# One core, two decoder blocks: the pooling mixer's padded chunks move to the convolution's tiles, and its modulation columns to its second half

## The chip, the cores and the metric

The kernel runs on one core of a Trainium2 chip. The metric is device time in microseconds (us) for one execution. A core has TensorE (matrix products, PE in the profile), VectorE (DVE), ScalarE (ACT), GpSimd (POOL) and SyncE (SP, which here only issues transfers). The engines run side by side, each works through its own instructions in the order in which the program holds them, and they wait for each other through semaphores.

## The reference

The input is one sequence of 512 tokens with 1024 channels. A first block applies two mixers to it, each behind a modulated norm; a second block applies attention, retention and a feed-forward part. Only the borders of the pooling mixer matter here. Cut to that:

```
sh, sc, gt = split(silu(c) @ w_mod[i] + b_mod[i])        # "modulation": one vector per block
h = rms(x, norm_g[i]) * (1 + sc) + sh

# mixer 0, convolution
a, b, g = split(h @ w_in);  y = depthwise_conv31(a * sigmoid(b)) + db
x += gt * ((silu(layernorm(y)) * silu(g)) @ w_out)

# mixer 1, pooling
v, g = split(h @ w_in)                                   # 1024 channels each
pooled = stack(window_mean(v_k, w) for w in (2, 4, 8, 16)) - v
y = (pooled @ w_grp per group) * scale
x += gt * ((y * silu(g)) @ w_out)
```

The second block's modulation is a product of the same kind, of its own vector silu(c_2) with 48 x 128 columns.

## The kernel before

Channels lie on the 128 partitions and the 512 tokens along them, so an activation of 1024 channels is eight tiles, called chunks here. Every matrix product is made of three TensorE passes, high half by high half, high by low and low by high: `mm3`, lines 307 to 309. Weights arrive in groups of eight 128 x 128 blocks (`w`, 512 KB); ScalarE makes the high half of a group (`whi`, line 291) and VectorE the low half (`wlo`, line 296). Three groups are held. `group_steps` writes these two instructions for the group that is two ahead of the one that TensorE reaches, so they stand in ScalarE's and VectorE's order at the start of each chunk.

**Pooling mixer.** Its input product has 16 output chunks of 24 matmuls each; chunks 0 to 7 are `v` and 8 to 15 are the gate. Chunks 0 to 2 are finished by the function `crossing`, and a loop makes 3 to 15, chunk by chunk, in four PSUM tiles in turn (two named `m`, two `z`). Weight group and chunk have the same number here. `ev_pl` takes a chunk out of PSUM: for chunks 0 to 7 ScalarE copies it (line 903) into a tile with eight zero columns at either end, which VectorE writes (lines 901 and 902), and `pool_chunk` makes running sums on GpSimd (line 888: one for window 2, two for 4, three for 8, four for 16), multiplies by the reciprocal count (GpSimd, line 891), subtracts the chunk (VectorE, line 892) and splits the result (VectorE, lines 379 and 380). For chunks 8 to 15 ScalarE applies the sigmoid-weighted gate (line 908). After chunk 15 come four groups of two outputs, 48 matmuls over two weight groups; `ev_g` takes each output out of PSUM on VectorE (line 920), and the output product follows (line 352 and on).

**Modulation columns.** `gemv` makes 128 of them: a transfer of 512 KB into one of two tiles `gw` (line 254) and a product with reduction on VectorE (line 255). 96 are needed in all, some called up at each step by `need`; the pooling mixer's loop calls for numbers 40 to 55, which are sixteen. Number 48 is the first that belongs to the second block: before its product the tile `cb` is loaded anew by a transfer that may start only when number 47's product is done (line 210), and ScalarE applies silu to it (line 211).

**Tiles.** The first two mixers share the pools of `Phase("A", ...)`. Pool `y` has four tiles: the convolution's padded inputs for VectorE and GpSimd, then the pooling mixer's padded chunks and its running sums. Pool `e` has 14 tiles of 272 numbers: for each of the five chunks that TensorE convolves two raw halves (line 649 on), two high and two low halves.

The engines' order in the convolution and the crossings is written by hand; in the pooling mixer's loop a scheduler sets it from the order of the code, the waits and its own estimates.

Of the kernel before, what the change touches and what calls it, by code (L numbers as in the profile page):

```python
# [9 lines left out]
F32 = mybir.dt.float32  # L10
F32R = mybir.dt.float32r
# [4 lines left out]
T = 512  # L16
# [115 lines left out]
def body(ctx: ExitStack, tc, ap, out):  # L132
# [12 lines left out]
    def nm(p):  # L145
        uid[0] += 1
        return f"{p}{uid[0]}"
# [11 lines left out]
        def close(self):  # L159
            self.stack.close()  # L160

    phase = [Phase("A", {"y": 4, "e": 14, "p": 2, "dg": 6, "v": 2, "c": 10, "a": 20, "z": 2, "d": 2})]

    def at(tag="a", dt=F32, n=T):
        return phase[0].pool[tag].tile([P, n], dt, tag=tag, name=nm(tag))
# [16 lines left out]
    def f(x):  # L182
        return x.bitcast(F32)

    mm = nc.tensor.matmul
    V, A, G = nc.vector, nc.scalar, nc.gpsimd
# [55 lines left out]
    done, pace = [0], [0]  # L242

    def gemv():
        i = done[0]
        if i >= 96:
            return
        done[0] += 1
        if i == 48:
            cb.append(silu_c("c_2"))  # L250
        j = MOD_ORDER[i]
        with tc.high_priority(offset=3000):
            t = gst.tile([P, D], F32, tag="g", name=nm("gw"))
            nc.sync.dma_start(out=t, in_=ap["wmod"][j])
        product = V.tensor_tensor_reduce(  # L255
            out=t, in0=t, in1=cb[-1], scale=1.0, scalar=bias_of(j),
            op0=ALU.mult, op1=ALU.add, accum_out=mod[:, j:j + 1])
        tc.keep_in_program_order(product)

    def need(n):  # L260
        while done[0] < n:
            gemv()
# [57 lines left out]
    def lin(src, ms, kn, evac, halves=False, acc=acc):  # L320

        if not halves:
            for m in ms:
                o = acc()
                for k in range(kn):
                    mm3(o, block(0), src[k], k == 0, k == kn - 1)
                    at_block[0] += 1
                evac(m, o, 0, T)
            return
        for a in (0, T // 2):  # L330
            b = a + T // 2
            for i, m in enumerate(ms):
                o = acc()
                for k in range(kn):
                    mm3(o[:, a:b], block(i * kn + k), cols(src[k], a, b), k == 0, k == kn - 1)
                evac(m, o, a, b)
        at_block[0] += len(ms) * kn
# [38 lines left out]
    def split_in(t, a=0, b=T, into=None, eng=None, n=T, tag="a"):  # L376

        hi, lo = into or (at(tag, F32R, n), at(tag, F32R, n))
        V.tensor_copy(out=hi[:, a:b], in_=t[:, a:b])
        (eng or V).tensor_tensor(out=lo[:, a:b], in0=t[:, a:b], in1=f(hi[:, a:b]), op=ALU.subtract)  # L380
        return hi, lo
# [171 lines left out]
    WE = H2 + 16  # L553
    ytile, yc, cv = {}, {}, {}
# [82 lines left out]
    def ev_in(m, o, a, b):  # L637
        if m < 8:
            pending[m] = o
            return  # L640
        if m < 16:
            i = m - 8
            s = at()
            A.activation(out=s, in_=o, func=AF.Sigmoid)  # L644
            v = pending.pop(i)
            if i in ON_PE:
                ytile[i] = []
                for g in range(2):
                    y = at("e", F32, WE)
                    V.memset(y[:, 0:8], 0.0)  # L650
                    V.memset(y[:, 7 + H2:WE], 0.0)
                    for p in range(2):
                        V.tensor_tensor(out=y[HALF[p], 7 + p:7 + p + H2], in0=v[HALF[g], p:T:2], in1=s[HALF[g], p:T:2], op=ALU.mult)
                    ytile[i].append(split_in(y, 0, WE, n=WE, tag="e"))
                return
            y = at("y", F32, WY)
            V.memset(y[:, 0:HALO], 0.0)
            V.memset(y[:, HALO + T:WY], 0.0)
            V.tensor_tensor(out=y[:, HALO:HALO + T], in0=v, in1=s, op=ALU.mult)
            ytile[i] = y  # L660
            return
        t = at()
        A.activation(out=t, in_=o, func=AF.Silu)
        pending[m] = t
# [134 lines left out]
    with tc.manual_schedule(engines=HAND):  # L799
# [29 lines left out]
        for _ in rsqrt_steps(pr(), [sq.acc], D, 0, T, n0.rb):  # L829
            next(work)  # L830
        lead[0] = 1
        lin_k(h0, CV_FIRST, KC, ev_in)
        lead[0], ahead[0] = LEAD, 1
        engine = {"V": V, "A": A, "G": G}
# [4 lines left out]
        for act in PLAN:  # L839
            kind, n, on = re.fullmatch(r"([a-z])(\d*)([A-Z]*)", act).groups()  # L840
            n = int(n or 1)
            if kind == "l":
                lin(n0.h, (n,), KC, lambda m, o, a, b: raw.update({m: o}), acc=pm)
            if kind == "x" or kind == "l" and n < 8:
                ev_in(n, raw.pop(n), 0, T)
            elif kind in running:
                for _ in range(n):
                    next(running[kind], 0)
            elif kind == "b":
                for _ in range(n):  # L850
                    early.append(diagonals(*later.pop(0), [engine[e] for e in on]))
            elif kind == "g":
                need(done[0] + n)
            elif kind == "c":
                conv_end(n, engine[on])
            elif kind == "s":
                next(stats)
            elif kind == "z":
                z_norm(n, engine[on])
            elif kind == "y":  # L860
                z_gate(n, *[engine[e] for e in on])
            elif kind == "m":
                next(products)
# [17 lines left out]
    def pool_chunk(m, v):  # L881
        w = WINDOWS[m // 2]

        W = T + 16
        cur, n = v, 1
        while n < w:
            s = at("y", F32, W)
            G.tensor_tensor(out=s[:, 0:W - 2 * n + 1], in0=cur[:, 0:W - 2 * n + 1], in1=cur[:, n:W - n + 1], op=ALU.add)
            cur, n = s, 2 * n
        t = at("c")  # L890
        G.tensor_tensor(out=t, in0=cur[:, 8 - w // 2:8 - w // 2 + T], in1=cnt[m // 2], op=ALU.mult)
        V.tensor_sub(out=t, in0=t, in1=v[:, 8:8 + T])
        pooled[m] = split_in(t)

    vt = {}

    def ev_pl(m, o, a, b):
        if m < 8:
            if m not in vt:
                vt[m] = at("y", F32, T + 16)  # L900
                V.memset(vt[m][:, 0:8], 0.0)
                V.memset(vt[m][:, 8 + T:16 + T], 0.0)  # L902
            A.copy(out=vt[m][:, 8 + a:8 + b], in_=o[:, a:b])
            if b == T:
                pool_chunk(m, vt.pop(m))
        else:
            t = at("dg" if m < 12 else "a")
            A.activation(out=t, in_=o, func=AF.Silu)
            sg[m - 8] = t

    for m, o in enumerate(first):
        ev_pl(m, o, 0, T)
    for m in range(len(first), 16):
        lin(n1.h, (m,), KC, ev_pl)
        need(done[0] + (2 if m < 6 else 1))
    z1 = [None] * KC

    def ev_g(m, o, a, b):
# [298 lines left out]
    def lin_tok():  # L1217

        os = [pz() if j < 2 else pm() for j in range(4)]
        for k in range(KC):  # L1220
            wh, wl = block(0, 4)
            at_block[0] += 4
            for j, o in enumerate(os):
                hh, hl = cols(h[k], j * P, j * P + P)
                mm(o, hh, wh, start=k == 0, stop=False)  # L1225
                mm(o, hh, wl, start=False, stop=False)  # L1226
                mm(o, hl, wh, start=False, stop=k == KC - 1)  # L1227
        return [split(o) for o in os]
# [99 lines left out]
    for hd in range(RET_HEADS):  # L1328
# [3 lines left out]
        v = lin_tok()  # L1332
# [168 lines left out]
```

## Time and profile before

| | us |
|---|---|
| median of 3 runs (lowest to highest) | 1681.62 (1677.55 to 1683.55) |
| the profiled execution's own time | 1682.93 |
| its span, first to last instruction | 1681.2 |
| TensorE busy in the span | 1601.3 (95%) |
| VectorE busy | 1036.3 (62%) |
| GpSimd busy | 500.6 (30%) |
| pooling mixer, chunk 3 to the first matmul of line 352 | 329.77 to 425.39 |

The span lacks the 1.7 us in which nothing of the core is recorded, before and after. Shares are means over stages with very different limits, so the stage's own rows count. In a timeline, a row is: start, duration, engine, line, operation, output from input, number merged, and in brackets the idle time ahead of it and what ended it.

### The profile page before, as it was taken

Reading aid. Unit: us, or ns where it says so; the run is one execution under the profiler, and the core shown is the slowest. Engines: PE = TensorE matmul, PEld = TensorE weight load, DVE = VectorE, ACT = ScalarE, POOL = GpSimd, SP = SyncE. Lnnn points to the kernel's source line nnn. Section 1 sums busy time; section 2 is a strip of 40 time slices with the busy share of each in tenths; the row PEclk is TensorE's granted clock in tenths of the full one; section 3 lists DMA queues with packets and bytes.
Section 4 is the critical chain, followed back from the end, with each engine's and each line's share of the span. In section 5 each row is a group of like instructions: output and inputs, shape, how many; then the busy total and the mean of one; then the engine's idle time right before and its main releaser. Section 6 shows DMA issues by size and latency. Waiting matters only on the chain.

```text
span 1681.2 us, 20261 instructions
## 1 busy us (share of the span) xinstructions
PE 1601.3 (95%) x7904; PEld 1351.6 (80%) x7904; DVE 1036.3 (62%) x1449; ACT 596.2 (35%) x920; POOL 500.6 (30%) x370
## 2 busy tenths in 40 slices
PE   6888898979999999999999999999999999999997
PEld 4677787968888878878888888888888888888887
DVE  6899988796678887886567554633254533333222
ACT  4422443523356566542332212223333422222221
POOL 2758635571124544550030201204441100000001
PEclk9999999989999999999999999999999999999999
DMA  8542334247521111225546332322322332332321
GB/s 273 163 151 68 109 126 144 76 150 248 191 76 51 52 62 51 72 67 165 167 153 203 95 118 71 96 89 74 99 91 85 101 92 96 100 100 90 99 89 62
DMA packets 54578, 187.64 MB, mean 112 GB/s; under 512 B 6097, under 2 KB 8273, under 8 KB 54482
## 3 DMA queue, kind: packets, MB, share of 16 engines
q1 hardware_dynamic: 52498, 183.20, 34.0%
q10 hardware_dynamic: 1984, 3.15, 0.6%
q8 instruction: 62, 1.02, 0.3%
q14 instruction: 34, 0.28, 0.1%
HBM read 184.22 MB, written 2.10 MB: 111 GB/s over the span
## 4 chain that ended last, share of the span: by engine, by line
PE 68%; DVE 18%; ACT 6%; issue 4%; POOL 3%; DMA 1%; SPq 0%; POOLq 0%; DVEq 0%; ACTq 0%
PE m L307 9%; PE m L308 9%; PE m L309 9%; PE z L307 7%; PE z L309 7%; PE z L308 7%; DVE wlo L296 4%; DVE gw L255 2%; DVE d L573 2%; ACT whi L291 1%; DVE dg L527 1%; PE m L1227 1%; PE z L1227 1%; PE z L1226 1%; PE m L1225 1%
## 5 line engine op out<-in xcount | busy, mean ns | idle before, releaser
L296 DVE TENSOR_TENSOR wlo<-w,whi 128x1024 fp32r<-128x1024 f32 (+1 forms) x243 | 329.8, 1360 | 341.4 <-ACT whi L291 340.5
L291 ACT CAST whi<-w 128x1024 fp32r<-128x1024 f32 x244 | 255.2, 1049 | 633.6 <-PE m L308 269.1
L307 PE MATMUL m<-h,whi 128*128 128x512 f32 x730 | 288.5, 395 | 4.6 <-ACT a L644 2.0
L309 PE MATMUL m<-h,wlo 128*128 128x512 f32 x730 | 286.5, 392 | 1.7 <-DVE y L902 1.4
L308 PE MATMUL m<-h,whi 128*128 128x512 f32 x730 | 286.1, 392 | 1.9 <-POOL h L480 1.9
L307 PEld LDWEIGHTS m<-h,whi 128*128 128x128 f32 x730 | 138.1, 189 | 36.0 <-ACT a L644 2.2
L309 PEld LDWEIGHTS m<-h,wlo 128*128 128x128 f32 x730 | 138.1, 189 | 32.3 <-DVE y L902 1.9
L308 PEld LDWEIGHTS m<-h,whi 128*128 128x128 f32 x730 | 137.8, 189 | 29.6 <-POOL h L480 2.2
L309 PE MATMUL z<-h,wlo 128*128 128x512 f32 x338 | 133.9, 396 | 7.1 <-DVE y L902 7.0
L307 PE MATMUL z<-h,whi 128*128 128x512 f32 x338 | 133.7, 395 | 0.0
L308 PE MATMUL z<-h,whi 128*128 128x512 f32 x338 | 133.2, 394 | 0.0
L397 POOL TENSOR_TENSOR c<-c,c 128x512 f32<-128x512 f32 x10 | 13.4, 1336 | 370.2 <-ACT c L435 370.0
L397 POOL TENSOR_TENSOR s<-s,s 128x512 f32<-128x512 f32 x14 | 18.7, 1333 | 321.0 <-ACT s L1265 292.2
L255 DVE CUSTOM_DVE_ANT_0 gw<-gw,cb,vec 128x1024 f32<-128x1024 f32 x64 | 92.2, 1448 | 20.3 <-DMA gw<-in_wmod 13.4
L1041 POOL TENSOR_TENSOR s<-s,s 128x512 fp32r<-128x512 f32 x64 | 92.7, 1458 | 30.7 <-DVE s L1040 30.7
L309 PE MATMUL z<-a,wlo 128*128 128x512 f32 (+1 forms) x222 | 81.7, 368 | 1.5 <-DVE wlo L296 1.5
L309 PEld LDWEIGHTS z<-h,wlo 128*128 128x128 f32 x338 | 64.7, 191 | 22.0 <-DVE y L902 7.8
L307 PE MATMUL z<-a,whi 128*128 128x512 f32 (+1 forms) x222 | 82.1, 370 | 0.0
L308 PE MATMUL z<-a,whi 128*128 128x512 f32 (+1 forms) x222 | 81.5, 367 | 0.0
L307 PEld LDWEIGHTS z<-h,whi 128*128 128x128 f32 x338 | 64.8, 192 | 13.3
L308 PEld LDWEIGHTS z<-h,whi 128*128 128x128 f32 x338 | 64.7, 191 | 13.4
L307 PE MATMUL m<-a,whi 128*128 128x512 f32 (+1 forms) x196 | 71.5, 365 | 0.0
(415 smaller groups left out, 3539.8 us busy)
## 6 DMA issues: line engine op xcount, KB each, us to landing
w<-in_weights SPq DMA_DIRECT2D x244, 512.0 KB, 3.7
gw<-in_wmod SPq DMA_DIRECT2D x96, 512.0 KB, 4.2
x<-in_xt SPq DMA_DIRECT2D x8, 256.0 KB, 4.5
s<-in_dec ACTq DMA_DIRECT2D x4, 256.0 KB, 3.6
out_x<-h SPq DMA_DIRECT2D x4, 256.0 KB, 2.5
p<-in_cnt ACTq DMA_DIRECT2D x2, 256.0 KB, 2.6
v<-in_cnt ACTq DMA_DIRECT2D x2, 256.0 KB, 3.2
cb<-in_c SPq DMA_DIRECT2D x1, 512.0 KB, 6.5
```

What stands on the lines that cost most here:

```text
L255: product = V.tensor_tensor_reduce(out=t, in0=t, in1=cb[-1], scale=1.0, scalar=bias_of(j), op0=ALU.mult, op1=ALU.add, accum_out=mod[:, j:j ...
L291: A.copy(out=hi, in_=w)
L296: e.tensor_tensor(out=lo[:, part], in0=w[:, part], in1=f(hi[:, part]), op=ALU.subtract)
L307: mm(o, l[0], r[0], start=first, stop=False)
L308: mm(o, l[0], r[1], start=False, stop=False)
L309: mm(o, l[1], r[0], start=False, stop=last)
L397: self.eng.tensor_tensor(out=n, in0=self.acc, in1=t, op=ALU.add)
L527: engs[s].tensor_tensor(out=t.rearrange("p (a b) -> p a b", a=8), in0=diag.unsqueeze(1).to_broadcast([P, 8, P // 2]), in1=dws[s][:, c:c + ...
L573: V.scalar_tensor_tensor(out=cv[i], in0=y[:, j:j + T], scalar=tap(i, j), in1=cv[i], op0=ALU.mult, op1=ALU.add)
L1041: G.tensor_tensor(out=lo[:, 0:w], in0=t[:, 0:w], in1=f(hi[:, 0:w]), op=ALU.subtract)
L1225: mm(o, hh, wh, start=k == 0, stop=False)
L1227: mm(o, hl, wh, start=False, stop=k == KC - 1)
```

## The change

The raw halves of the TensorE convolution go to pool `c` (ten tiles, shared with norms and the convolution's results), and a high and a low half share one tile of pool `e`, which now has seven tiles of 544 numbers. The pooling mixer's padded chunks go to `e`, and `y` keeps the running sums alone. The loop over chunks 3 to 15 calls for no modulation column up to chunk 7 and for two after each of chunks 8 to 15 (before: two after chunks 3 to 5, one after each later one); there are sixteen either way. From line 650 on, lines of the changed kernel stand one higher.

```
-    phase = [Phase("A", {"y": 4, "e": 14, "p": 2, "dg": 6, "v": 2, "c": 10, "a": 20, "z": 2, "d": 2})]
+    phase = [Phase("A", {"y": 4, "e": (7, 2 * 272), "p": 2, "dg": 6, "v": 2, "c": 10, "a": 20, "z": 2, "d": 2})]
...
-                    y = at("e", F32, WE)
+
+                    y, e = at("c"), at("e", F32R, 2 * WE)
...
-                    ytile[i].append(split_in(y, 0, WE, n=WE, tag="e"))
+                    ytile[i].append(split_in(y, 0, WE, into=(e[:, 0:WE], e[:, WE:2 * WE])))
...
-                vt[m] = at("y", F32, T + 16)
+                vt[m] = at("e", F32, T + 16)
...
-        need(done[0] + (2 if m < 6 else 1))
+        need(done[0] + (2 if m >= 8 else 0))
```

VectorE's order in the first half, before, from the low half of weight group 6 to that of group 7. The L892 row subtracts chunk 3, and the two L379 and L380 rows split it; each `gw` row is a modulation column.

```order
L296 TENSOR_TENSOR wlo_3014<-w_2959,whi_3013 128x1024
L901 MEMSET y_3041 128x8
L902 MEMSET y_3041 128x8
L892 TENSOR_TENSOR c_2997<-c_2997,y_2989 128x512
L379 CAST a_3000<-c_2997 128x512
L380 TENSOR_TENSOR a_3001<-c_2997,a_3000 128x512
L255 ISA gw_3004,mod<-gw_3004,cb_144,vec 128x1024
L255 ISA mod 128x1
L255 ISA gw_3007,mod<-gw_3007,cb_144,vec 128x1024
L255 ISA mod 128x1
L296 TENSOR_TENSOR wlo_3068<-w_3011,whi_3067 128x1024
```

The same place in the changed kernel:

```order
L296 TENSOR_TENSOR wlo_2998<-w_2949,whi_2997 128x1024
L893 TENSOR_TENSOR c_2987<-c_2987,e_2979 128x512
L379 CAST a_2990<-c_2987 128x512
L380 TENSOR_TENSOR a_2991<-c_2987,a_2990 128x512
L296 TENSOR_TENSOR wlo_3046<-w_2995,whi_3045 128x1024
```

The two columns are gone from between the two weight groups, and so are the memsets, which now stand in the convolution. The same five rows follow for chunks 4, 5 and 6; the first two columns come behind the low half of group 10.

VectorE's order at the end of the loop, before, from the low half of the first `w_grp` group (`wlo_3447`) to the first output of `ev_g` (L920):

```order
L296 TENSOR_TENSOR wlo_3447<-w_3408,whi_3446 128x1024
L255 ISA gw_3476,mod<-gw_3476,cb_3257,vec 128x1024
L255 ISA mod 128x1
L296 TENSOR_TENSOR wlo_3483<-w_3444,whi_3482 128x1024
L255 ISA gw_3512,mod<-gw_3512,cb_3257,vec 128x1024
L255 ISA mod 128x1
L296 TENSOR_TENSOR wlo_3519<-w_3480,whi_3518 128x1024
L920 SCALAR_TENSOR_TENSOR c_3528<-m_3515,vec,dg_3255 128x512
```

The same stretch in the changed kernel, where `wlo_3431` belongs to the first `w_grp` group:

```order
L296 TENSOR_TENSOR wlo_3431<-w_3389,whi_3430 128x1024
L255 ISA gw_3424,mod<-gw_3424,cb_3379,vec 128x1024
L255 ISA mod 128x1
L255 ISA gw_3460,mod<-gw_3460,cb_3379,vec 128x1024
L255 ISA mod 128x1
L296 TENSOR_TENSOR wlo_3470<-w_3428,whi_3469 128x1024
L255 ISA gw_3463,mod<-gw_3463,cb_3379,vec 128x1024
L255 ISA mod 128x1
L255 ISA gw_3499,mod<-gw_3499,cb_3379,vec 128x1024
L255 ISA mod 128x1
L296 TENSOR_TENSOR wlo_3509<-w_3467,whi_3508 128x1024
L255 ISA gw_3502,mod<-gw_3502,cb_3379,vec 128x1024
L255 ISA mod 128x1
L921 SCALAR_TENSOR_TENSOR c_3518<-m_3505,vec,dg_3221 128x512
```

Five columns stand there where two stood, and the last of the sixteen is the row just ahead of the first output of `ev_g`.

ScalarE's order around the new `cb`, in the changed kernel (`whi_3391` is the high half of weight group 15, `m_3346` is chunk 12):

```order
L909 ACTIVATE dg_3338<-z_3307 128x512
L211 ACTIVATE cb_3379<-cb_3379 128x1024
L909 ACTIVATE a_3377<-m_3346 128x512
L291 CAST whi_3391<-w_3347 128x1024
```

Before, `cb` stood behind the gate of chunk 9 and ahead of the high half of weight group 13; now it stands behind that of chunk 11 and ahead of the high half of group 15.

## Rows read from the trace of the kernel before

**Rows 1.** The page's first part: TensorE's busy time, share and instructions.
```profile
PE 1601.3 (95%) x7904; PEld 1351.6 (80%) x7904; DVE 1036.3 (62%) x1449; ACT 596.2 (35%) x920; POOL 500.6 (30%) x370
```

**Rows 2.** Windows: length, busy time by engine, TensorE's granted clock, DMA share.
```profile
351.61:381.21 29.60, 21.16 (x74) 16.14 (x72) 29.29 (x33) 4.81 (x7) 21.46 (x15) 0.83 0.56 173
...
414.51:425.39 10.88, 10.88 (x50) 9.01 (x48) 10.03 (x14) 6.08 (x9) 3.99 (x3) 1.00 0.65 226
```

**Rows 3.** TensorE's timeline, chunks 7 to 10 and the output product's first matmul.
```profile
355.24 0.80 PE L309 MATMUL z<-h,wlo 128*128 128x512 f32 x1 [3.02 <-DVE y L902]
355.83 0.63 PE L307 MATMUL z<-h,whi 128*128 128x512 f32 x1
...
363.91 0.50 PE L309 MATMUL m<-h,wlo 128*128 128x512 f32 x1 [1.45 <-DVE y L902]
...
373.63 0.80 PE L309 MATMUL z<-h,wlo 128*128 128x512 f32 x1 [3.98 <-DVE y L902]
...
381.21 0.39 PE L307 MATMUL m<-h,whi 128*128 128x512 f32 x1
...
425.39 0.39 PE L352 MATMUL m<-a,whi 128*128 128x512 f32 x1
```

**Rows 4.** VectorE's timeline, low halves of groups 6 and 7 and between them.
```profile
342.18 2.09 DVE L296 TENSOR_TENSOR wlo<-w,whi 128x1024 fp32r<-128x1024 f32 x1
...
346.40 1.54 DVE L892 TENSOR_TENSOR c<-c,y 128x512 f32<-128x512 f32 x1 [2.09 <-POOL c L891]
347.97 1.17 DVE L379 CAST a<-c 128x512 fp32r<-128x512 f32 x1
349.18 1.42 DVE L380 TENSOR_TENSOR a<-c,a 128x512 fp32r<-128x512 f32 x1
350.52 2.31 DVE L255 CUSTOM_DVE_ANT_0 gw<-gw,cb,vec 128x1024 f32<-128x1024 f32 x1
...
353.97 1.22 DVE L296 TENSOR_TENSOR wlo<-w,whi 128x1024 fp32r<-128x1024 f32 x1
```

**Rows 5.** GpSimd: its wait for padded chunks (300 to 400 us), and its timeline.
```profile
POOL y L888 <- DVE y L902: 11.0, 4, 3.8
...
355.36 4.04 POOL L888 TENSOR_TENSOR y<-y 128x527 f32<-128x527 f32 x3 [3.61 <-DVE y L902]
...
373.75 6.27 POOL L888 TENSOR_TENSOR y<-y 128x527 f32<-128x527 f32 x4 [1.26 <-DVE y L902]
380.10 2.16 POOL L891 TENSOR_TENSOR c<-y,p 128x512 f32<-128x512 f32 x1
```

**Rows 6.** VectorE's timeline, second half of the loop and the first output of `ev_g`.
```profile
394.58 1.29 DVE L255 CUSTOM_DVE_ANT_0 gw<-gw,cb,vec 128x1024 f32<-128x1024 f32 x1 [6.93 <-ACT cb L211]
...
399.64 1.29 DVE L255 CUSTOM_DVE_ANT_0 gw<-gw,cb,vec 128x1024 f32<-128x1024 f32 x1 [1.42 <-DMA gw<-in_wmod]
...
416.71 0.75 DVE L920 SCALAR_TENSOR_TENSOR c<-m,vec,dg 128x512 f32<-128x512 f32 x1
```

**Rows 7.** Timelines of SP's queue and of ScalarE: the new `cb`.
```profile
386.92 0.43 SPq L210 DMA_DIRECT2D cb<-in_c  x1
...
393.49 1.06 ACT L211 ACTIVATE cb<-cb 128x1024 f32<-128x1024 f32 x1 [10.77 <-DMA cb<-in_c]
```

**Rows 8.** Transfers issued at 395.9, 397.1, 408.5 and 386.9: size, issue to landing.
```profile
gw<-in_wmod SPq DMA_DIRECT2D x1, 512.0 KB, 3.6
...
gw<-in_wmod SPq DMA_DIRECT2D x1, 512.0 KB, 4.2
...
gw<-in_wmod SPq DMA_DIRECT2D x1, 512.0 KB, 5.5
...
cb<-in_c SPq DMA_DIRECT2D x1, 512.0 KB, 6.5
```

**Rows 9.** TensorE in the convolution: a wait, and the window behind it.
```profile
123.72 0.58 PE L307 MATMUL z<-e,dg 128*128 128x256 f32 x1 [5.64 <-DVE dg L527]
...
123.70:129.70 6.00, 5.98 (x27) 5.83 (x28) 5.97 (x4) 2.87 (x4) 5.92 (x4) 0.50 0.39 131
```

## The prediction

> **What bounds the kernel now.** The page's first part comes first: TensorE is busy for 95% of the span [rows 1], so the most that any edit can win lies in the few places where it stands still or runs below its full clock. The second look is the granted clock by windows [rows 2]: from 351.61 to 381.21 it is 0.83 and TensorE is busy for 21.16 of 29.60 us, while VectorE is busy for 29.29; from 414.51 to 425.39 TensorE is busy throughout at 1.00. Third, TensorE's timeline [rows 3] says where the loss sits: waits of 3.02, 1.45 and 3.98 us ahead of the low half of a weight group, for chunks 7, 8 and 9. The first is put down to a memset (line 902) that had long been done; the low half `wlo` on VectorE starts at 353.97 and takes 1.22 [rows 4], so it ends at 355.19, and TensorE goes on at 355.24.
>
> What is lost can be counted. Chunk 10 starts at 381.21 and line 352 at 425.39 [rows 3]. The last stretch holds 48 matmuls in 10.88 us [rows 2], 0.2267 each, so a chunk of 24 takes 5.44. From 381.21, six chunks and that stretch should take 43.52, and took 44.18: only 0.66 is lost late. Chunks 7 to 9 should take 16.32 and took the 29.60 of the first window: 13.28 lost, 8.45 in the three waits and 4.83 in a clock below full behind the two longer ones (0.83 over the window).
>
> VectorE is late because its work for a chunk, beside GpSimd, is `wlo` 2.09, L892 1.54, the cast 1.17, line 380 1.42, and two columns of up to 2.31 [rows 4]: 8 to 9 us against 5.44. And it also waits 2.09 for GpSimd there, which for its part waits 11.0 in all for padded chunks [rows 5], since in the old order the memsets into a `y` tile stand behind VectorE's other work.
>
> **The change, early part: tiles and columns.** The convolution keeps its instructions; its raw halves lie in another pool, and eight pairs of memsets join it on VectorE, where they wait until TensorE has read an `e` tile. A pass over 512 columns costs 1.17 [rows 4] and eight columns are a 64th of it, so the work is near 0, under a TensorE that is busy 95% of the span [rows 1]. Of the waits I know the bounds alone: nothing where VectorE comes later than TensorE, and the 5.64 of a wait in the convolution [rows 9] where it comes first, with the rest of VectorE's evictions queued behind. I take 0, because TensorE's convolution of a chunk is over before VectorE splits the next in the order of the code, and leave the other end to the slower rival below. The four-fold wait of GpSimd (11.0 us, [rows 5]) goes. Its last instruction ended at 382.26 (380.10 plus 2.16); without waits that is 371.3. Chunk 7's own sums and product are 6.27 plus 2.16, so chunk 6 is done there at 362.8.
>
> VectorE then never waits for GpSimd long, and runs beside it nearly always. One period is 1.54 + 1.17 + 1.42 + 2.09 = 6.22 us [rows 4], against TensorE's 5.44. The low half of group 6, at 342.18, comes later: some six instructions ahead of it, which ran beside an idle GpSimd, now run beside a busy one, and each loses about what `wlo` does (2.09 less 1.22, 0.87), some 4.7 us in all, less than 6 x 0.87 because the shorter ones lose less. That ends it near 349.0, and four more periods of 6.15 to 6.22 bring the first column to 373.6 at the latest; bounded from below it is chunk 6's end plus a period, 369.0. I take C = 372.5, nearer the upper end because the rows show contention in each instruction. TensorE reads a low half some 0.6 us into a chunk (355.24 less 3.02 is 352.22, chunk 7 began at 351.61), so it starts chunk 10 at about 371.6, **9.6 us earlier** than 381.21. Its 3.7 us above seven bare chunks from 329.77 come in waits of 0.6 to 2 us, and the 1.45 of chunk 8 left the clock at full.
>
> **The late part: sixteen columns behind one another.** All have to be done between C and the first L920, which in the new order stands right behind the last. A product takes 1.2 to 1.29 [rows 6]. A tile freed at 395.87 was read again at 399.64, and loads took 3.6 and 4.2, once 5.5 [rows 8]; so I count 4.1 us from a product's end to the next product on that tile (3.6 and 4.2, each with the 0.15 us between landing and reading). The products from C on, each with its end:
>
> - 1 and 2 (loaded ahead): C+2.4; chunk 7's finish 1.8 (L892 and the split, without GpSimd), a `wlo` of 1.2: C+5.4. Numbers 3 and 4 end at C+6.6 and +7.8, `wlo` +9.0.
> - 5 and 6: read at +10.7 (6.6 + 4.1) and +11.9, ending at +13.1; `wlo` +14.3. 7 and 8: +17.2 and +18.4.
> - Then `cb`. Its transfer may start only now: 0.5 for the issue (row 0.43), 6.57 from issue at 386.92 to silu at 393.49, silu 1.06 [rows 7]. S = C+26.5, that is 399.0. Both engines get past it: ScalarE has the high half of group 15 behind it.
> - 9 and 10: S+2.4; `wlo` of group 15 S+3.6 = 402.6. TensorE reaches chunk 15 at 371.6 + 5 x 5.44 = 398.8, so it waits some 3.4 for it and ends it at about 407.6.
> - 11: S+6.5, `wlo` +7.7, 12: +8.9; 13: +11.8, `wlo` +13.0, 14: +14.2; 15 waits for its load: +17.1, `wlo` +18.3, 16: +19.5, which is C+46.0 = **418.5**.
>
> Behind it L920 takes 0.75 [rows 6]. Four PSUM tiles take the outputs 0 to 3 (5.44 us, to 413.0); the fifth waits for the first L920, until 419.2, 6.2 us. A wait of 5.64 left half clock, 0.50, for the next 6.00 us [rows 9], so nearly half of such a stretch is lost: 2.8, and the four outputs left cost 5.44 + 2.8. TensorE reaches line 352 at 419.2 + 8.2 = 427.5, against 425.39: **+2.1 us**. What is won early is paid back in the eight last chunks.
>
> The profiled execution took 1682.93 with a span of 1681.2, and stands 1.31 above the median of 1681.62. 1682.93 + 2.1 = 1685.0; on the median's scale 1683.7. Five waits for a load lie on the path (5, 7, 11, 13, 15). The lower bounds together, C at 369.0 and loads of 3.6 all told, give 3.5 + 2.5 = 6.0 less, 1677.7; the upper ones, C at 373.6 and the mean of the three loads (4.4 and 0.15), 1.1 + 2.25 = 3.4 more, 1687.1.
>
> The Trainium skill has a rule against the price of contention that I took ("SBUF — State Buffer", section "Who interferes with whom"): the port pair that VectorE and GpSimd share is an exclusive lock, and the loser is fully blocked. By it a VectorE instruction could wait for a whole GpSimd instruction, here 1.57 us (6.27 over 4, [rows 5]), and with three or four such waits the period would be near 9 us, C 385 and the sum +14.6. The row has `wlo` at 2.09 against 1.22 [rows 4], a loss of 0.87, so the trace shows less than a full block, and it decides.
>
> **The rivals.**
>
> *Faster: the loads nearly hide.* At 3.2 us from product to product, and 5.2 for `cb`, the same list gives S = C+23.4, the `wlo` of group 15 at 399.5 and the sixteenth product's end at C+40.2 = 412.7. TensorE loses 0.7 at chunk 15, has four outputs done at 410.4 and waits until 413.45, 3.05 us. If the clock bears that (1.45 it bore, 3.02 it did not, [rows 2, 3]), or C lies at its lower end, line 352 comes at 418.9 or 418.2, 6.5 to 7.2 earlier: **1675**. For it: the early part wins 9.6 in any case. Against it: the fastest load shown took 3.6 and that of `cb` 6.5 [rows 8]. It decides, beyond 0.3%, from the two together. Chance 0.18. The Trainium skill ("DMA: Bandwidth & Descriptors", section "Anatomy of one DMA — SWDGE (gpsimd) path") gives a transfer about 2.0 us fixed and 436 GB/s on GpSimd's path, by which I estimate 3.2 us for 512 KB; the rows' 3.6 to 5.5 do not agree with it.
>
> *Slower: the loads are long.* One took 5.5 [rows 8], and the tail asks for more than before: sixteen columns and eight weight groups of 512 KB in 46 us are 273 GB/s, against 226 in the last window at 0.65 of the DMA engines [rows 2]. With all at 5.65 to the product, five steps are each 1.55 longer, 7.75, and line 352 comes 9.9 later than before: **1691.5**. It decides from 4.7, where five steps of 0.6 make +2.1 into +5.1. Against it: two of three loads were shorter. Chance 0.20.
>
> *Slower: the waits of GpSimd stay.* That the change does not do what it says: if the padded chunks in `e` wait for something else, or the convolution pays for the memsets, C stays where the old waits put it, chunk 6 done near 372.5 and C at 378.7, and all of the late part 6.2 later: +8.3, **1689.9**. The convolution's 5.64 would come to about the same. Against it: the convolution, which alone shares `e`, is over before chunk 3. Chance 0.08.
>
> **How the numbers follow.** The forecast holds 0.54, the fast case 0.18, the slow ones 0.28. 0.3% of 1682 is 5.0 us, about what a measurement of this kernel can tell from no change; +2.1 lies within it, and so does most of the forecast's own range, 1677.5 to 1687. So: faster 0.18, same 0.54, slower 0.28. The range of 8 in 10 reaches from there to the near side of the fast case and takes in the third rival and the nearer half of the second: 1676 to 1690.5.
>
> **What would show it.** GpSimd's waits for padded chunks gone and its last instruction of the stage near 371; VectorE without a column from 342 to 372, with `wlo` 6.2 us apart; no wait of TensorE above 2.5 us up to chunk 10, which starts at 371 to 373. Then: `cb` issued near 391, silu near 398; a wait of TensorE of 3 to 4 us ahead of chunk 15; the last column right ahead of the first L920, at 418 to 419; a wait of some 6 us ahead of the fifth output, with half clock behind it; line 352 near 427.5. Wrong would be: the low halves 8 us apart as before (contention by the skill's rule), columns' loads of 3 us or 5, or the first L920 before 413, when the tail costs nothing and the early gain stays.

## The result and the profile after

The changed kernel takes 1691.84 us (median of 6, 1688.86 to 1695.72) against 1682.51 (median of 6) of the kernel before in the same session; the ratio is 1.0063, interval 1.0045 to 1.0081. It is slower by some 0.6%, or 9 to 10 us, where +2.1 us was forecast, and lies above the forecast's range of 1676 to 1690.5. Its profiled execution has a span of 1691.5, that of before 1681.2.

Windows of the changed kernel (columns as in [rows 2]): the time in which chunks 7 to 9 ran before, the time from there to the groups, and a short one behind a wait of TensorE at chunk 5:

```profile
351.61:381.21 29.60, 28.41 (x124) 22.92 (x123) 27.72 (x23) 8.51 (x12) 21.57 (x14) 1.00 0.40 124
381.21:414.51 33.30, 28.43 (x112) 22.08 (x111) 17.79 (x25) 6.90 (x9) 0.00 (x0) 0.90 0.73 242
...
344.18:348.18 4.00, 4.00 (x11) 3.13 (x12) 4.00 (x5) 0.00 (x0) 3.77 (x4) 0.57 0.42 131
```

The first window, where TensorE was busy for 21.16 us before, has it busy for 28.41 at full clock. The loss moved into the second window. TensorE's timeline shows where:

```profile
344.18 0.50 PE L309 MATMUL z<-h,wlo 128*128 128x512 f32 x1 [1.96 <-DVE wlo L296]
...
372.68 0.39 PE L307 MATMUL m<-h,whi 128*128 128x512 f32 x1
373.84 0.50 PE L309 MATMUL m<-h,wlo 128*128 128x512 f32 x1 [0.55 <-DVE wlo L296]
...
405.73 0.54 PE L307 MATMUL z<-h,whi 128*128 128x512 f32 x1 [3.49 <-ACT whi L291]
407.99 0.79 PE L309 MATMUL z<-h,wlo 128*128 128x512 f32 x1 [1.29 <-DVE wlo L296]
...
426.14 0.79 PE L307 MATMUL m<-a,whi 128*128 128x512 f32 x1 [5.15 <-DVE c L921]
...
433.48 0.39 PE L352 MATMUL m<-a,whi 128*128 128x512 f32 x1
```

The three waits of [rows 3] are gone. In their place stand one at chunk 5 (1.96), two at chunk 15 (3.49 and 1.29, 405.73 and 407.99) and one ahead of the fifth output of the groups (5.15). Chunk 10 begins at 372.68, not 381.21; line 352 at 433.48, not 425.39.

VectorE's timeline, with the low halves of groups 5 and 10, columns 1, 5, 7 and 8, then 9 (the first with the new `cb`), 16, and the first output:

```profile
342.01 2.11 DVE L296 TENSOR_TENSOR wlo<-w,whi 128x1024 fp32r<-128x1024 f32 x1
...
371.47 2.31 DVE L296 TENSOR_TENSOR wlo<-w,whi 128x1024 fp32r<-128x1024 f32 x1
373.71 2.31 DVE L255 CUSTOM_DVE_ANT_0 gw<-gw,cb,vec 128x1024 f32<-128x1024 f32 x1
...
386.95 1.28 DVE L255 CUSTOM_DVE_ANT_0 gw<-gw,cb,vec 128x1024 f32<-128x1024 f32 x1 [2.67 <-DMA gw<-in_wmod]
...
392.60 1.28 DVE L255 CUSTOM_DVE_ANT_0 gw<-gw,cb,vec 128x1024 f32<-128x1024 f32 x1 [1.66 <-DMA gw<-in_wmod]
...
394.44 1.28 DVE L255 CUSTOM_DVE_ANT_0 gw<-gw,cb,vec 128x1024 f32<-128x1024 f32 x1 [0.54 <-DMA gw<-in_wmod]
...
404.30 1.28 DVE L255 CUSTOM_DVE_ANT_0 gw<-gw,cb,vec 128x1024 f32<-128x1024 f32 x1 [7.43 <-ACT cb L211]
...
424.13 1.28 DVE L255 CUSTOM_DVE_ANT_0 gw<-gw,cb,vec 128x1024 f32<-128x1024 f32 x1 [1.20 <-DMA gw<-in_wmod]
...
425.34 0.75 DVE L921 SCALAR_TENSOR_TENSOR c<-m,vec,dg 128x512 f32<-128x512 f32 x1
```

From the first column (373.71) to the first output behind the sixteenth (425.34) are 51.63 us; the prediction's list had 46.0. VectorE waits for data in most of it. SP's queue and ScalarE around the new `cb`, and the transfers issued from 370 to 427 (size, median from issue to landing):

```profile
396.14 0.42 SPq L210 DMA_DIRECT2D cb<-in_c  x1
...
403.20 1.06 ACT L211 ACTIVATE cb<-cb 128x1024 f32<-128x1024 f32 x1 [16.35 <-DMA cb<-in_c]
404.17 0.58 ACT L909 ACTIVATE a<-m 128x512 f32<-128x512 f32 x1
404.64 1.98 ACT L291 CAST whi<-w 128x1024 fp32r<-128x1024 f32 x2
```
```profile
gw<-in_wmod SPq DMA_DIRECT2D x16, 512.0 KB, 4.5
w<-in_weights SPq DMA_DIRECT2D x9, 512.0 KB, 4.6
cb<-in_c SPq DMA_DIRECT2D x1, 512.0 KB, 6.7
```

ScalarE stands 16.35 us at the silu of `cb`, and the gate of chunk 12 and the high half of group 15 stand behind it: that is TensorE's 3.49. A column's load takes 4.5 us, where the prediction had worked from 3.6 and 4.2 [rows 8].

GpSimd no longer waits for VectorE's memsets [rows 5], but once, for 3.10 us, for ScalarE's copy of a chunk that TensorE finished late. Its last product ends at 374.93, where the prediction had 371:

```profile
352.50 1.84 POOL L889 TENSOR_TENSOR y<-e 128x527 f32<-128x527 f32 x1 [3.10 <-ACT e L904]
...
372.78 2.15 POOL L892 TENSOR_TENSOR c<-y,p 128x512 f32<-128x512 f32 x1
```

### The profile page after: what moved, and what is told of

The parts are those of the page before. It is cut to its first block, busy times and chain, and to the rows that moved or that the text cites. A ratio compares the mean times of both kernels' runs of the same rounds, so it can differ in the third digit from the quotient of the medians.

```text
span 1691.5 us, 20258 instructions
## 1 busy us (share of the span) xinstructions
PE 1602.4 (95%) x7904; PEld 1349.2 (80%) x7904; DVE 1040.9 (62%) x1449; ACT 595.4 (35%) x920; POOL 501.2 (30%) x370
## 4 chain that ended last, share of the span: by engine, by line
PE 63%; DVE 20%; ACT 6%; issue 4%; DMA 4%; POOL 3%; SPq 0%; POOLq 0%; DVEq 0%; ACTq 0%
PE m L307 8%; PE m L308 8%; PE m L309 8%; PE z L309 7%; PE z L307 7%; PE z L308 7%; DVE wlo L296 5%; DMA gw<-in_wmod 2%; DVE gw L255 2%; DVE d L573 2%; ACT whi L291 1%; DVE dg L527 1%; PE z L1227 1%; PE m L1228 1%; PE z L1226 1%
## 5 line engine op out<-in xcount | busy, mean ns | idle before, releaser
L296 DVE TENSOR_TENSOR wlo<-w,whi 128x1024 fp32r<-128x1024 f32 (+1 forms) x243 | 333.9, 1376 | 342.5 <-ACT whi L291 341.5
L255 DVE CUSTOM_DVE_ANT_0 gw<-gw,cb,vec 128x1024 f32<-128x1024 f32 x64 | 88.1, 1382 | 26.4 <-DMA gw<-in_wmod 19.0
```

The source lines that it names most:

```text
L255: product = V.tensor_tensor_reduce(out=t, in0=t, in1=cb[-1], scale=1.0, scalar=bias_of(j), op0=ALU.mult, op1=ALU.add, accum_out=mod[:, j:j ...
L296: e.tensor_tensor(out=lo[:, part], in0=w[:, part], in1=f(hi[:, part]), op=ALU.subtract)
```

## The experiments

The start of chunk 3 lies between 327.8 and 333.9 in the profiles of the kernels below, also among those with the same program ahead of it, so places in the stage are given from that start. Three are used: the start of chunk 10, line 352, and the first matmul of the right half of the crossing behind the output product (line 767 to 769, which waits some 1.9 us for ScalarE in every kernel but one_each). Behind the crossing the profiles of the table hold 1202 to 1210 us, 1207.8 before and in the change; no run shows what makes that spread, so a place in the stage says more than one profile's total. Ratios are to the kernel before, with their 95% interval.

| kernel | chunk 10 | line 352 | crossing | median us | ratio |
|---|---|---|---|---|---|
| before | 51.4 | 95.6 | 143.7 | 1680.3 to 1682.5 by session | |
| the change | 42.0 | 102.8 | 153.1 | 1691.84 | 1.0063 (1.0045 to 1.0081) |
| tiles_alone | 55.0 | 98.5 | 146.7 | 1687.39 | 1.0034 (1.0018 to 1.0050) |
| columns_alone | 41.1 | 104.3 | 153.9 | 1691.81 | 1.0057 (1.0036 to 1.0078) |
| one_each | 43.3 | 87.1 | | 1795.71 | 1.0683 (1.0654 to 1.0713) |
| no_cb | 43.3 | 98.3 | 146.5 | 1682.95 | 1.0011 (0.9992 to 1.0030) |
| own_cb | 42.1 | 99.2 | 148.0 | 1684.33 | 1.0019 (1.0007 to 1.0032) |
| half_gw | 42.0 | 90.3 | 138.6 | 1676.39 | 0.9973 (0.9961 to 0.9986) |
| first_in_y | 41.0 | 103.4 | 152.8 | 1692.21 | 1.0076 (1.0060 to 1.0091) |
| balanced | 43.3 | 87.6 | 144.8 | 1682.06 | 1.0011 (0.9999 to 1.0024) |
| split_14_10 | 42.0 | 90.2 | 142.1 | 1679.11 | 0.9995 (0.9979 to 1.0010) |
| split_15_9 | 42.1 | 95.2 | 144.0 | 1678.72 | 0.9990 (0.9971 to 1.0009) |
| tiles_first_in_y | 55.2 | 98.7 | 147.3 | 1686.45 | 1.0028 (1.0012 to 1.0045) |

**tiles_alone: one half of the change** (edit of the changed kernel, as all below but columns_alone).

```diff
-        need(done[0] + (2 if m >= 8 else 0))
+        need(done[0] + (2 if m < 6 else 1))
```

> The tiles as in the changed kernel, the columns called up as before (two after chunks 3 to 5, one after each later one). Theory T (the late column chain is the loss): the new tiles cost nothing, GpSimd's wait for padded chunks goes, but VectorE still has its columns in the first half and stays the limit there with some 8.5 us a chunk, so the start of chunk 10 moves by less than 3 us from 381.21 and the total is 1682.5 within 4 us either way. Rival U (the tiles are the loss, because VectorE now runs beside a GpSimd that never pauses): slower by 5 us or more, 1688 and up, with the waits of TensorE ahead of chunk 10.

Measured: the tiles alone make it slower, between the two theories' bounds in total, and by U's mechanism: chunk 10 starts 55.0 behind chunk 3, 3.5 later than before. TensorE's waits:

```profile
346.46 0.50 PE L309 MATMUL z<-h,wlo 128*128 128x512 f32 x1 [1.93 <-DVE wlo L296]
...
370.40 0.80 PE L309 MATMUL m<-h,wlo 128*128 128x512 f32 x1 [4.80 <-DVE wlo L296]
...
381.19 0.50 PE L309 MATMUL z<-h,wlo 128*128 128x512 f32 x1 [2.89 <-DVE wlo L296]
```

A new wait at chunk 5, and then 4.80 and 2.89 where [rows 3] had 3.02, 1.45 and 3.98. VectorE's low halves of groups 7 and 8 took 1.22 each before ([rows 4] has the first), while GpSimd stood in two of the waits of [rows 5]. Here GpSimd works through, and the same two take:

```profile
357.69 2.07 DVE L296 TENSOR_TENSOR wlo<-w,whi 128x1024 fp32r<-128x1024 f32 x1
...
368.07 2.27 DVE L296 TENSOR_TENSOR wlo<-w,whi 128x1024 fp32r<-128x1024 f32 x1
```

So the pauses of GpSimd, with which the new tiles did away, had let VectorE run at full speed.

**columns_alone: the other half** (edit of the kernel before).

```diff
-        need(done[0] + (2 if m < 6 else 1))
+        need(done[0] + (2 if m >= 8 else 0))
```

> The tiles as before, the sixteen columns in chunks 8 to 15. Theory T: the same late chain as in the changed kernel (some 52 us from the first product to the first output of the groups), starting where chunk 7's work ends, and VectorE relieved in the first half; slower than before by 7 to 16 us, 1690 to 1698. Rival U: without the new tiles there is no loss, 1682.5 within 4 us.

Measured: as T had it, 1691.81. The early gain is whole without the new tiles, chunk 10 at 41.1, and the late loss too:

```profile
407.58 0.50 PE L307 MATMUL z<-h,whi 128*128 128x512 f32 x1 [3.46 <-ACT whi L291]
409.84 0.80 PE L309 MATMUL z<-h,wlo 128*128 128x512 f32 x1 [1.34 <-DVE wlo L296]
...
428.85 0.80 PE L307 MATMUL m<-a,whi 128*128 128x512 f32 x1 [5.99 <-DVE c L920]
```

So the columns decide. By one profile each, the tiles add some 3 us at line 352 with the columns in the first half, and take 1.4 with them in the second.

**no_cb: the second vector's transfer left out** (columns 48 to 95 are made with the first vector).

```diff
-        if i == 48:
+        if i == -1:
             cb.append(silu_c("c_2"))
```

> The changed kernel with the second vector's cb left out: columns 48 to 95 are made with the first vector's cb, so the work left out is one transfer of 512 KB and one silu. Theory T: the list loses the 8.1 us from the issue of cb to the end of its silu; the wait of TensorE for chunk 15 (3.49 and 1.29) goes, the sixteenth product ends near 417, the fifth output of the groups still waits 5 to 7 us with half clock behind it, and line 352 comes at 426 to 427, 8 us earlier; total 1683.5 within 3 us. If cb were only a part that other loads hide, the gain is under 3 us: 1689 and up. Rival U: under 2 us.

Measured: 1682.95, 8.9 below the changed kernel and not to be told from the kernel before. By place it is less: line 352 comes 4.6 earlier, not 8, which is 4.6 of the 7.2 lost there, and the crossing 6.6 of 9.4; the profile's other 5 us lie behind the crossing, within the spread there. The waits:

```profile
404.59 0.50 PE L309 MATMUL z<-h,wlo 128*128 128x512 f32 x1 [0.53 <-DVE wlo L296]
...
423.14 0.80 PE L307 MATMUL m<-a,whi 128*128 128x512 f32 x1 [7.33 <-DVE c L921]
```

Chunk 15's wait is gone. TensorE comes to the fifth output sooner and waits 7.33 there for the sixteenth column: the list, 46.4 us without `cb` for 51.6 with it, still ends too late. Of the 8.1 us expected 5.2 came, for the later columns still wait for their own loads. In the output product it gets back 2 us more (crossing 48.2 behind line 352, against 50.2 in the changed kernel and 48.0 before).

**own_cb: the second vector in its own tile, loaded early.**

```diff
-    phase = [Phase("A", {"y": 4, "e": (7, 2 * 272), ... "a": 20, "z": 2, "d": 2})]
+    phase = [Phase("A", {"y": 3, "e": (7, 2 * 272), ... "a": 19, "z": 2, "d": 2, "f": 1})]
...
-        cb.append(const.tile([P, D], F32, tag="cb", name=nm("cb")))
+        cb.append(at("f", F32, D))
...
-            cb.append(silu_c("c_2"))
+            cb.extend(cb2)
...
+        if m == 4:
+            cb2.append(silu_c("c_2"))
```

The edit also moves the gates of chunks 12 and 13 from `a` to `dg` tiles, since `a` has one fewer, and holds the silu at its place in the program's order.

> The changed kernel, but the second vector gets a tile of its own (the first vector's lies in a pool of the first two mixers, which gives up one a tile and one y tile for it), so that its transfer runs early and its silu stands behind the copy of chunk 4. Theory: the new cb in the middle of the column chain is what makes TensorE wait at chunk 15, so the result is that of the run in which it was left out, 1683 within 3 us, with line 352 some 98 us after the start of chunk 3 and no wait at chunk 15 over 1 us. Rival (the eight columns behind the cb wait for their own loads just as long): line 352 stays 101 us or more behind chunk 3, 1688 and up.

Measured: 1684.33, as expected, with no wait over 0.5 us at chunk 15; it is still 0.19% slower than before. What is left is the same wait as in no_cb:

```profile
419.82 0.80 PE L307 MATMUL m<-a,whi 128*128 128x512 f32 x1 [7.41 <-DVE c L923]
```

**half_gw: half the bytes of the sixteen columns** (the other half of their sums is left out).

```diff
+            n = D // 2 if 40 <= i < 56 else D
-            nc.sync.dma_start(out=t, in_=ap["wmod"][j])
+            nc.sync.dma_start(out=t[:, 0:n], in_=ap["wmod"][j][:, 0:n])
...
-            out=t, in0=t, in1=cb[-1], scale=1.0, scalar=bias_of(j),
+            out=t[:, 0:n], in0=t[:, 0:n], in1=cb[-1][:, 0:n], scale=1.0, scalar=bias_of(j),
```

> The changed kernel with columns 40 to 55 made from half of their rows: transfers of 256 KB and products over 512 numbers; the other half of these sixteen sums is left out. Theory that the bytes of the loads set the list: a load takes near 3.2 us in place of 4.5, a column 2.0 in place of 2.75, the list is 10 to 13 us shorter, the wait for the fifth output is under 3 us and the total 1680 to 1684. Rival (a load's time is mostly fixed, whatever its size): loads stay over 4 us, only the products are shorter, the list shrinks by 3 to 6 us, 1686 to 1689.

Measured: 1676.39, below both bounds given and below the kernel before. Line 352 comes 12.5 us earlier than in the changed kernel, though `cb` is still in the chain. The loads from 375 to 416, and the one late wait left:

```profile
gw<-in_wmod SPq DMA_DIRECT2D x14, 256.0 KB, 3.3
```
```profile
416.98 0.66 PE L308 MATMUL m<-a,whi 128*128 128x512 f32 x1 [1.97 <-DVE c L922]
```

3.3 us for 256 KB and 4.5 for 512 KB: the second 256 KB cost 1.2 us, and a straight line through the two medians leaves 2.1 that don't hang on the size. The Trainium skill ("DMA: Bandwidth & Descriptors", section "Anatomy of one DMA — SWDGE (gpsimd) path") has 2.0 us fixed for transfers that GpSimd issues. SyncE issues these, and their 2.1 agrees; the 436 GB/s of the Trainium skill is double what a load got here beside another load and the weights (256 KB in 1.2 us, 218 GB/s). The products were halved as well (0.75 for 1.28), so not all of the 12.5 is the loads'. With two tiles in turn a column takes half of a load and a product together: by that estimate 2.9 us whole and 2.0 halved, and some two thirds of the difference are the load's.

**one_each: eight columns in the loop, sixteen in the output product.**

```diff
-        need(done[0] + (2 if m >= 8 else 0))
+        need(done[0] + (1 if m >= 8 else 0))
```

> The changed kernel with one column after each of chunks 8 to 15 in place of two, so that the other eight and the new cb come in the output product, whose steps call for two each. Theory T: chunk 10 starts near 373 as in the changed kernel, no wait of TensorE over 2 us follows up to line 352, which comes at 416 to 418, 17 us earlier than in the changed kernel; the output product with sixteen columns and the new cb gives back 3 to 12 of them; total 1678 to 1687. Rival U: no earlier than 1689.

Measured: line 352 as T had it, 87.1 behind chunk 3 (before 95.6), and the total a miss by 110 us. The silu of the new `cb` now ran behind the hand-written load of the other function table. ScalarE's timeline, and its table loads by line:

```profile
416.72 1.28 ACT L931 ACT_TABLE_LOAD   x1
...
419.08 1.28 ACT L211 ACT_TABLE_LOAD   x1
420.37 1.06 ACT L211 ACTIVATE cb<-cb 128x1024 f32<-128x1024 f32 x1
```
```profile
L1076 ACT ACT_TABLE_LOAD x48 | 61.6, 1283 | 0.9
L1075 ACT ACT_TABLE_LOAD x34 | 43.6, 1283 | 0.6
...
L1105 ACT ACT_TABLE_LOAD x15 | 19.2, 1283 | 0.3
```

The row of line 931 is that hand-written load. From there on the second block's exponentials and logarithms, which had found one table for both (the kernel before has no table load in them), change tables 97 times, 124 us of ScalarE. The run says nothing on the forecast's tail but for line 352, and that the output product's columns make TensorE wait 5.93 for a low half behind it.

**first_in_y: chunk 3's padded chunk back in y.**

```diff
-                vt[m] = at("e", F32, T + 16)
+                vt[m] = at("y" if m < 4 else "e", F32, T + 16)
```

> The changed kernel, but the padded chunks 0 to 3 lie in pool y as before; chunks 4 to 7 stay in e. Theory (VectorE is late at chunk 5 because GpSimd no longer pauses beside it): GpSimd pauses again for chunk 3, the low half of group 5 comes early enough, the wait of 1.96 at chunk 5 and the half clock behind it, 3.9 us together, go; some of that is given back where chunk 3's own sums come later, so chunk 10 starts 38 to 41 us behind chunk 3 (42.05 in the changed kernel), and the total is 1 to 4 us lower, 1688 to 1691. Rival (the low half of group 5 is late for its high half or its weights): the wait at chunk 5 stays at 1.9, and chunk 10 at 42.

Measured: the wait at chunk 5 went, as the theory had it, so it was GpSimd's company that made the low half late. But chunk 10 starts only 1.0 earlier and line 352 is 0.5 later: in total nothing (1692.21, where 1688 to 1691 was expected). The wait and the half clock at chunk 5, 3.9 us for that chunk, are nearly all made good by chunk 10, since VectorE's low halves set the pace of the chunks between.

**balanced, split_14_10, split_15_9: twelve, fourteen or fifteen columns in the loop**, the rest in the output product, all with own_cb's tile.

```diff
-        need(done[0] + (2 if m >= 8 else 0))
+        need(done[0] + (1 + m % 2 if m >= 8 else 0))              # balanced
+        need(done[0] + (0 if m < 8 else 2 if m < 14 else 1))      # split_14_10
+        need(done[0] + (0 if m < 8 else 2 if m < 15 else 1))      # split_15_9
```

> The second vector in a tile of its own as in own_cb, and in chunks 8 to 15 one column behind the even and two behind the odd chunks: twelve there and twelve in the output product. Theory (a column costs 2.75 us as long as two tiles take turns): 12 x 2.75 = 33 is less than the 43.5 that TensorE needs for the eight chunks, so line 352 comes 87 to 90 us after the start of chunk 3 (before: 95.6); the output product's twelve take 33 of its 36 us, so no more than 3 are given back there; total 1674 to 1679, faster than both kernels. Rival (the output product can't take twelve: where it had sixteen, the crossing behind it came 22 us late): line 352 as early, but the crossing 5 or more us late, 1682 and up.

> As balanced, but two columns behind each of chunks 8 to 13 and one behind 14 and 15: fourteen there, ten in the output product. Theory (the balanced run lost its gain where the last low halves of the output product stand behind the last columns; two columns fewer there are 5.5 us of loads less, and fourteen in the loop, 38.5 us, still end before the first output of the groups is needed): line 352 again 87 to 89 us after the start of chunk 3, no wait over 2 us at the end of the output product, total 1674 to 1678, faster than both kernels. Rival (the early gain is lost there whatever the split, because something else than the columns is late): 1681 and up.

> As balanced, but fifteen columns in chunks 8 to 15 (one behind chunk 15, two behind the others) and nine in the output product. Theory: the list in the loop is 2.75 us longer than with fourteen and ends about when the fifth output of the groups is due, so TensorE waits there for 0 to 4 us, with half clock behind it if for over 2; line 352 88 to 94 us after chunk 3, nothing lost later, total 1674 to 1682, not better than with fourteen. Rival: better than fourteen by over 2 us, if the output product's columns are still what costs.

Measured: balanced has line 352 8.0 us earlier than before, and at the crossing it is 1.2 later, the rival's outcome (1682.06). The place is the end of the output product, where a low half stands behind the last columns:

```profile
457.50 0.58 PE L309 MATMUL r<-a,wlo 128*128 128x256 f32 x1 [4.32 <-DVE wlo L296]
```

With fourteen that wait is gone, and the list waits a little in the groups instead (1.43 there); with fifteen 4.17, and half clock (0.50 over the next 4 us), so that line 352 comes at 95.2, past the 88 to 94 expected. Fourteen is 1.5 us ahead of the kernel before at the crossing, but in total neither it (0.9995) nor fifteen (0.9990) can be told from it. The 1674 to 1678 expected of fourteen was not reached: line 352 came at 90.2, not 87 to 89, and the stretch to the crossing takes 51.9, for 48.0 before.

**tiles_first_in_y: the same edit as first_in_y, in tiles_alone.**

> The tiles alone (columns called up as before), but padded chunks 0 to 3 in y as before. Theory (with the columns in the first half, the tiles cost because VectorE runs beside an unpaused GpSimd and its low half is late at chunk 5): the wait of 1.93 at chunk 5 and its half clock go, chunk 10 starts 50 to 53 us behind chunk 3 (tiles alone 55.0, before 51.4), total within 3 us of the kernel before. Rival (the loss moves on to the chunks behind, as it did in the changed kernel with the same edit): chunk 10 starts 54 us or more behind chunk 3, total 4 us or more above the kernel before.

Measured: the rival's outcome. The wait at chunk 5 is gone and chunk 10 starts at 55.2, as late as without the edit; the total is 0.28% above before (5.3 us by the medians of its session), past the 4 us that the rival set. The loss moved on to chunk 7, where TensorE now waits 4.65. The columns and the contended work of chunks 3 to 7 are more than VectorE can do in time, wherever the first wait lies.

## Why the prediction was wrong, step by step

**What bounds the kernel: right.** VectorE's low halves set chunks 5 to 9, and with the columns out the waits of [rows 3] went.

**The early part: right in size, wrong in its cause.** Chunk 10 was forecast at 371.6 and came at 372.68, the first column at 372.5 and came at 373.71; the start of chunk 3 was 0.88 later in this execution, which leaves 0.2 and 0.3. That it fits so closely is in part luck. The forecast had four periods of 6.2 us from the low half of group 6 on; they were 4.0, 5.3, 6.4 and 7.6 (low halves at 348.18, 352.20, 357.48, 363.86 and 371.47). The first two are short: while GpSimd stood 3.10 us for ScalarE's copy, VectorE's subtraction, cast, line 380 and the next low half took 0.68, 0.43, 0.69 and 1.22 us, where the forecast had 1.54, 1.17, 1.42 and 2.09. The last holds a wait of VectorE for GpSimd. But the prediction let the tiles share in the gain, by way of GpSimd's 11.0 us of waits [rows 5]. columns_alone has the whole gain without them (41.1), and tiles_alone none (55.0). GpSimd's waits were no loss: they were the time in which VectorE ran uncontended. The sum also took a wait of up to 2 us as free of the clock; 1.96 at chunk 5 halved it (0.57 in the window), 9.3 us for that chunk, of which first_in_y shows 1.0 left at chunk 10.

**The late part: the mechanism was right, the loads were mis-sized.** This is the step that failed: "I count 4.1 us from a product's end to the next product on that tile". Number 5 was read 13.2 behind the first column (386.95 less 373.71), not 10.7; number 7 18.9, not 16.0; the eighth ended at 22.0, not 18.4; the silu of `cb` ended 30.6 behind, not 26.5; the sixteenth ended at 51.6, not 46.0. From a product's end to the next product on that tile were 3.7 to 5.4 us where the product waited for its load, 4.6 in the mean of ten. The 4.1 came from two of the three rows of [rows 8]; the third, 5.5, went into the upper bound alone, and the mean of the three, 4.4, is nearly the 4.5 that came. Of the 5.6 us that the list ran longer, some 4 are these waits, 1.1 are the first column, which took 2.31 beside GpSimd's last product where the list had 1.2, and 0.4 are `cb`. half_gw shows that the loads' bytes set much of the pace: with half of them, and half the product, line 352 is 12.5 us earlier. Why the loads took longer than before stays open. The kernel before moved as much or more when its loads were short (from 380 to 416 us 253 GB/s with the DMA engines 73% busy, for 231 and 70% from 370 to 427 here):

```profile
gw<-in_wmod SPq DMA_DIRECT2D x9, 512.0 KB, 4.0
```

With 1.2 us from C (0.9 of it the later start of chunk 3) and 5.6 from the list, less 0.9 that TensorE got back in the shorter wait (7.34 from the fifth output to line 352, for 8.2), line 352 came 6.0 later than the 427.5 forecast.

**What was left out:** the output product. The prediction ended at line 352, as if all behind it moved by as much. From there to the crossing are 50.2 us, against 48.0 before. The other runs have 48.2 to 57.2 there. It goes with how many columns the stretch itself holds (57.2 us with twelve, 51.9 with ten, 48.8 with nine) and, with eight, with the columns ahead of it (49.5 to 50.2 in the runs whose fifth output is latest, 48.2 in no_cb). In the changed kernel TensorE has two waits there that the kernel before had not:

```profile
434.44 0.50 PE L352 MATMUL m<-a,whi 128*128 128x512 f32 x1 [0.34 <-DVE c L921]
...
462.07 0.50 PE L353 MATMUL d<-a,wlo 128*128 128x512 f32 x1 [0.87 <-DVE wlo L296]
```

The first is for an output of the groups; the second is for a low half that stands behind a column whose load came 1.98 us late.

The sum of the two profiles: 0.9 ahead of chunk 3, 7.2 to line 352, 2.2 to the crossing, together the 10.3 by which the spans differ. The first is within what executions of one program differ by there.

**The rivals.** The second one's time (1691.5) is nearly that measured, and its cause, longer loads, is most of the cause; but that the number fits is luck, since its steps of 5.65 were not there (4.6 in the mean), and a part of the time came from the output product, on which it had nothing. The first (hidden loads) fell with the loads' 4.5. The third fell: GpSimd's waits for padded chunks did go, and the memsets in the convolution left no mark that can be told from the spread at chunk 3's start. Only seven of the eight pairs stand there: pool `e` has seven tiles for eight padded chunks, and the last pair comes in the loop, at 346.75, where nothing waits for it. The Trainium skill's exclusive lock ("SBUF — State Buffer", section "Who interferes with whom") made no period of 9 us: the longest step between low halves is the 7.6 above. That the trace shows less than a full block, as the prediction read it, is not shown, though: a low half of 2.31 beside 1.22 lost 1.09, and GpSimd's passes over 527 numbers took some 1.06 at their shortest, so the loss is about one of them.

What stays open: why the loads were longer than before, and the 1 us of the output product's 2.2 that its two waits do not hold.

## What to carry to other kernels

When work is moved to where its engine is idle, count the transfers that feed it, with the duration that they have when as many run at once as will: sixteen loads through two tiles set a pace of their own (2.9 us a column in no_cb, half of a load and a product together), whatever the engine could do. An engine's wait for another may be what keeps the other at full speed; take it away alone before it is booked as a gain. And follow a delay past the end of the stage that is changed, and a moved activation function past the table load that it now stands behind.

## What the runs showed of the hardware that was not expected

The same wait of TensorE at chunk 5, 1.91 to 1.96 us, halved the clock behind it in six profiles (the change, tiles_alone, own_cb, half_gw and both splits: chunk 5 took 9.3 us) and left it at full in three (no_cb, one_each, balanced: 7.7 us). The 4.00 us behind it in no_cb, to be held against the 0.57 of the changed kernel above:

```profile
345.71:349.71 4.00, 4.00 (x18) 3.30 (x19) 4.00 (x5) 0.00 (x0) 3.77 (x4) 1.00 0.40 131
```

So a wait of this length has no one price: 2.2 or 3.9 us for the chunk. Here the dearer case cost nothing in the end: chunk 10 starts 42.0 to 42.1 behind chunk 3 in the five profiles with half clock and late columns, and 43.3 in the three at full clock.

With one activation in the wrong place, 97 of 144 later exponentials and logarithms had a table load of 1.28 us ahead of them, and the total was 115 us above the kernel before (one_each).
